# Where tiles lie in the on-chip memory: operands of TensorE at the low end, raw weights and the residual at the high end

## The chip, the cores and the metric

The kernel runs on one core of a Trainium2 chip. The metric is the device time of one execution, in microseconds (us), as the median of several runs. Profiles come from one execution each, recorded by the hardware profiler; their span runs from the first to the last instruction.

## The reference

One decoder layer on x of 256 rows (positions) and 2048 columns, in float32:

```python
x = x + 0.5 * swiglu_ffn(rms_norm(x, ffn1_norm), w_gate, w_up, w_down)   # 2048 -> 5632 -> 2048
z = rms_norm(x, mix_norm) @ w_in                                        # 2048 -> 5120
...   # half of z: width-4 conv, gated linear recurrence, GeLU gate; the rest: gated width-3 conv
x = x + concat(rms_norm(y_lru), rms_norm(y_sc)) @ w_out
x = x + 0.5 * swiglu_ffn(rms_norm(x, ffn2_norm), w_gate, w_up, w_down)
return rms_norm(x, final_norm)
```

with `swiglu_ffn(x) = (silu(x @ w_gate) * (x @ w_up)) @ w_down`. All weights, about 340 MB, are read once.

## The kernel before, in words

**Split products.** The inputs are float32 and TensorE multiplies in a rounded format (float32r). So each operand is split in two: `hi` is its rounded copy (made by ScalarE, `act.copy`), `lo` is what is left (made by VectorE, a subtraction). A product is hi·hi + lo·hi + hi·lo, three matmuls in place of one. A weight block is a *unit* of 512 x 512 numbers: `load` (L155) brings it from HBM into a raw tile of 128 partitions x 4 x 512, 8 KB in each partition; `parts_of` (L169) makes its `hi` and its `lo`, 8 KB each; `multiply` (L194) runs the matmuls. In an FFN and in w_out the rows of x are loaded as the stationary operand, 128 x 128, and the weights are streamed, 512 columns at a time: for one product with a tile of 128 rows a unit gives 8 matmuls with `hi` and 4 with `lo`, 12 in all; 24 if it serves two products. In w_in (`columns`) it is the other way round: the weights are stationary and x is streamed.

**The stages.** FFN 1, the mixer with w_in and w_out, FFN 2. In each FFN the first 512 columns of gate and up are multiplied unit by unit (8 units of 24 matmuls). The other columns go through `seven`, which computes a 2 x 2 arrangement of blocks in seven products instead of eight (Strassen's way): weight blocks are added and subtracted by VectorE in place (`raw_g<-raw_g,raw_g` in the profile), then split and multiplied by sums of the activation blocks. Products over the remaining row blocks (`usual`) are added to the same banks. With two such blocks a `seven` has 7 units of 12 matmuls and 4 of 24, with one it has 7 and 2. Five rounds of gate and up, each a `seven` of two blocks, are followed after the first, third and fifth by `down`: a part of w_down, for two of its four column groups by plain `product` (2 x 3, 2 x 4 and 2 x 4 units of 24), for the other two by a `seven` with one, two and two extra blocks. Between them the hidden activations are transposed by TensorE (`ph`) and split. In the names of the profile `_p` marks one of the seven products, `_x` a `usual` one, and a/c/d/e the bank.

**Order of the work.** Each engine runs its instructions in order. SyncE issues the loads of raw tiles as those tiles come free; the numbers of buffers bound how far the loads and the splitting run ahead of TensorE. Small pieces of other work (transpositions for the next norm, the recurrence) are deferred and handed out by `pump` between units.

**The pools.** All tiles lie in the on-chip memory, 224 KB in each partition, in pools that are opened one after another on one stack, each behind the one before:

- `const`: xres (the residual, 16 KB), the identity, small vectors. L74.
- `raws`: three raw tiles, 24 KB. L75.
- `splits`: two sets of `hi` and `lo`, 32 KB. L76.
- `bigs`: ten tiles of 8 KB, 80 KB: the split activations that TensorE loads as stationary (xT, x, xs, h, yT), and some others. L77.
- `work`: scratch of the norms, some 6 KB. L78.
- then one pool for the stage: in an FFN `ffn1` or `ffn2` with 13 `keep` tiles of 2 KB (sums of banks, activations, and in a `down` the split sums `hs`, which TensorE loads), a third set of `hi` and `lo` with one buffer each (16 KB), and two `kept` raw tiles (16 KB); in the mixer `mixer` and `mixw` in the same place.

While an FFN's pool is open (`extra` isn't empty) every third call of `parts_of` takes the third set. The count, `turn_of["split"]`, runs on from FFN 1 to FFN 2; the mixer uses `splits` alone:

```python
        pool, bufs = splits, 2
        if extra:
            turn_of["split"] += 1
            if turn_of["split"] % 3 == 0:
                pool, bufs = extra[0], 1
```

A raw tile in an FFN goes to `kept` for the first two blocks of a `seven`, and for two of five units of a plain product.

Of the kernel before, what the change touches and what calls it, by code (L numbers as in the profile page):

```python
# [10 lines left out]
F32 = mybir.dt.float32  # L11
# [5 lines left out]
P = 128  # L17
D = 2048
S = 256
FF = 5632  # L20
NT = S // P
# [27 lines left out]
def hybrid_block(ctx: ExitStack, tc: tile.TileContext, a: dict, out: bass.AP):  # L49
# [21 lines left out]
            fn()  # L71
            owed[0] -= cost

    const = ctx.enter_context(tc.tile_pool(name="const", bufs=1))  # L74
    raws = ctx.enter_context(tc.tile_pool(name="raws", bufs=3))  # L75
    splits = ctx.enter_context(tc.tile_pool(name="splits", bufs=2))  # L76
    bigs = ctx.enter_context(tc.tile_pool(name="bigs", bufs=10))  # L77
    work = ctx.enter_context(tc.tile_pool(name="work", bufs=2))  # L78
    psum = ctx.enter_context(tc.tile_pool(name="psum", bufs=8, space=bass.MemoryType.PSUM))

    def bank(name):
# [3 lines left out]
        return ap.bitcast(F32)  # L85


    xres = const.tile([P, NT, D], F32, name="xres")

    def load_x(c):  # L90
        cs = slice(c * CW, (c + 1) * CW)
# [309 lines left out]
        done(0, 0, d, [s1])  # L401

    def ffn(tag, norm, after, opening=False):
        with tc.tile_pool(name=f"ffn{tag}", bufs=1) as fp:
            extra.append(fp)
            turn_of["hold"] = True
            wg, wu, wd = (a[f"ffn{tag}_w_{s}"][0] for s in ("gate", "up", "down"))
# [64 lines left out]
            left = []  # L472
# [169 lines left out]
    def to_mixer(c, t):  # L642
# [3 lines left out]
        else:  # L646
            held["nm"].later(c)

    ffn(1, n1, to_mixer, True)
    nm = held["nm"]  # L650


    with tc.tile_pool(name="mixer", bufs=1) as mp, tc.tile_pool(name="mixw", bufs=2) as mw:
        wgate = {}

        def gate_weights(key, src):
# [218 lines left out]
    def last(c, t):  # L875
# [31 lines left out]
        for engine, begin, end in ((act, 0, 256), (dve, 1536, 2048), (act, 256, 768), (dve, 768, 1536)):  # L907
# [8 lines left out]
            nc.sync.dma_start(ov[:, t, o], xo)  # L916

    ffn(2, n2, last)


# [28 lines left out]
```

## Time and profile before

| what | value |
|---|---|
| median of 3 runs | 1754.29 us (1753.98 to 1757.33) |
| the profiled execution: time, span | 1759.12 us, 1757.3 us |
| granted TensorE clock | 0.998 |
| VectorE busy, ScalarE busy | 1491.3 us, 1050.3 us |
| DMA | 343.24 MB, mean 195 GB/s |

The profile names a tile without its buffer number, so a unit in the third set has the same name as one in `splits`. All helpers' instructions stand at one line, L42, the wrapper that issues them. A row of the timeline gives the start of a group of equal instructions, the time from its first start to its last end, the engine, the operation, the tile written, those read (of a matmul the streamed operand, then the stationary one), the shape and the count. As matmuls overlap at their ends, the pace of a group is the start of the next group less its own start, divided by the count. The last but two columns of a stage's row (`1.00 0.57 195`) are the granted clock, the share of the DMA engines and GB/s; ahead of them stand, for each engine, its busy time and number of instructions.

### The profile page before, as it was taken

The numbers are of one execution on the slowest core, as the hardware profiler recorded it, in microseconds if no ns is written. First come the engines' busy times: TensorE is split into PE (matmuls) and PEld (weight loads), VectorE is DVE, ScalarE is ACT, GpSimd is POOL, SyncE is SP. The second block draws the span as 40 slices with busy tenths as digits, with TensorE's granted clock in tenths as the row PEclk, the third lists the DMA queues.
The fourth block names the chain that finished last, engine by engine and source line by source line (L and its number), as shares of the span: only waits on it lengthen the run. The fifth ranks groups of instructions, "written<-read, shape, count | busy, mean of one in ns | idle before, by whom it ended". The sixth has DMA issues, their size and how long they took to land. (4 is left out here: it accounts for less than half of the span.)

```text
span 1757.3 us, 20323 instructions
## 1 busy us (share of the span) xinstructions
PE 1735.2 (99%) x8031; PEld 1434.5 (82%) x8031; DVE 1491.3 (85%) x1240; ACT 1050.3 (60%) x1366; POOL 6.9 (0%) x32
## 2 busy tenths in 40 slices
PE   8999999999999999999999999999999999999997
PEld 7778788888888888888888888888788888888876
DVE  6998989889789898588986668989799887899885
ACT  7665565655465666565765455656556654556654
POOL 1000000000000000000000000000000000000000
PEclk9999999999999999999999999999999999999999
DMA  8365655575556555456555664575475646555742
GB/s 313 119 231 176 216 192 193 191 263 185 169 198 203 200 195 194 166 169 193 186 180 185 241 204 131 205 247 177 162 248 201 208 145 225 191 192 192 254 172 102
DMA packets 173904, 343.24 MB, mean 195 GB/s; under 512 B 5620, under 2 KB 8048, under 8 KB 173680
## 3 DMA queue, kind: packets, MB, share of 16 engines
q1 hardware_dynamic: 173344, 340.82, 57.3%
q8 instruction: 63, 1.03, 0.2%
q10 hardware_dynamic: 144, 1.05, 0.1%
q14 instruction: 33, 0.27, 0.0%
q0 software_dynamic: 320, 0.07, 0.0%
HBM read 339.82 MB, written 2.10 MB: 195 GB/s over the span
## 5 line engine op out<-in xcount | busy, mean ns | idle before, releaser
L42 PE MATMUL ps_in<-xT_nm,hi_in 128*128 128x512 f32 x640 | 224.0, 395 | 0.0
L42 ACT CAST hi_g_p<-raw_g 128x1024 fp32r<-128x1024 f32 x140 | 142.3, 1049 | 110.8 <-DVE raw_g L42 53.9
L42 DVE TENSOR_TENSOR lo_g_p<-raw_g,hi_g_p 128x2048 fp32r<-128x2048 f32 x70 | 159.7, 2287 | 31.2 <-ACT hi_g_p L42 30.9
L42 ACT CAST hi_u_p<-raw_u 128x1024 fp32r<-128x1024 f32 x140 | 141.1, 1049 | 74.3 <-DVE raw_u L42 27.9
L42 PE MATMUL ps_in<-xT_nm,lo_in 128*128 128x256 f32 x640 | 178.7, 281 | 1.6 <-DVE lo_in L42 1.6
L42 DVE TENSOR_TENSOR lo_u_p<-raw_u,hi_u_p 128x2048 fp32r<-128x2048 f32 x70 | 159.1, 2286 | 19.3 <-ACT hi_u_p L42 19.0
L42 PE MATMUL ps_d<-hi_d,h 128*128 128x512 f32 x704 | 169.5, 392 | 0.0
L42 PEld LDWEIGHTS ps_d<-hi_d,h 128*128 128x128 f32 x704 | 131.5, 188 | 28.2
L42 PEld LDWEIGHTS ps_in<-xT_nm,hi_in 128*128 128x128 f32 x640 | 119.8, 187 | 27.1
L42 ACT CAST hi_d<-raw_d 128x1024 fp32r<-128x1024 f32 x88 | 88.3, 1049 | 69.8 <-PE ps_u_d L42 20.1
L42 DVE TENSOR_TENSOR lo_d<-raw_d,hi_d 128x2048 fp32r<-128x2048 f32 x44 | 100.6, 2291 | 32.0 <-ACT hi_d L42 32.0
L42 PEld LDWEIGHTS ps_in<-xT_nm,lo_in 128*128 128x128 f32 x640 | 120.6, 189 | 2.6 <-DVE lo_in L42 2.4
L42 DVE TENSOR_TENSOR lo_in<-raw_in,hi_in 128x2048 fp32r<-128x2048 f32 x40 | 91.4, 2285 | 32.9 <-ACT hi_in L42 27.6
L42 ACT CAST hi_in<-raw_in 128x1024 fp32r<-128x1024 f32 x80 | 81.6, 1050 | 62.5 <-PE ps_in L42 48.4
L42 ACT CAST hi_d_p<-raw_d 128x1024 fp32r<-128x1024 f32 x84 | 84.3, 1047 | 54.0 <-DVE raw_d L42 38.6
L42 ACT CAST hi_g_x<-raw_g 128x1024 fp32r<-128x1024 f32 x80 | 81.5, 1049 | 43.9 <-PE ps_g_c L42 24.4
L42 DVE TENSOR_TENSOR lo_d_p<-raw_d,hi_d_p 128x2048 fp32r<-128x2048 f32 x42 | 95.5, 2288 | 13.5 <-ACT hi_d_p L42 13.4
L42 ACT CAST hi_u_x<-raw_u 128x1024 fp32r<-128x1024 f32 x80 | 80.5, 1049 | 35.6 <-PE ps_u_c L42 21.2
L42 DVE TENSOR_TENSOR raw_u<-raw_u,raw_u 128x2048 f32<-128x2048 f32 x40 | 91.5, 2290 | 11.4 <-DMA raw_u<-in_ffn_w_up_dram 10.8
L42 DVE TENSOR_TENSOR raw_g<-raw_g,raw_g 128x2048 f32<-128x2048 f32 x40 | 91.4, 2287 | 8.4 <-DMA raw_g<-in_ffn_w_gate_dram 7.9
L42 DVE TENSOR_TENSOR lo_g_x<-raw_g,hi_g_x 128x2048 fp32r<-128x2048 f32 x40 | 91.5, 2286 | 4.4 <-ACT hi_g_x L42 4.3
L42 DVE TENSOR_TENSOR lo_u_x<-raw_u,hi_u_x 128x2048 fp32r<-128x2048 f32 x40 | 91.4, 2285 | 1.0 <-ACT hi_u_x L42 0.3
(347 smaller groups left out, 3602.2 us busy)
## 6 DMA issues: line engine op xcount, KB each, us to landing
raw_u<-in_ffn_w_up_dram SPq DMA_DIRECT2D x88, 1024.0 KB, 5.3
raw_d<-in_ffn_w_down_dram SPq DMA_DIRECT2D x88, 1024.0 KB, 5.1
raw_g<-in_ffn_w_gate_dram SPq DMA_DIRECT2D x87, 1024.0 KB, 5.2
raw_in<-in_w_in_dram SPq DMA_DIRECT2D x40, 1024.0 KB, 5.1
raw_o<-in_w_out_dram SPq DMA_DIRECT2D x16, 1024.0 KB, 5.0
xres<-in_x_dram SPq DMA_DIRECT2D x4, 512.0 KB, 8.1
fin<-in_final_norm_dram ACTq DMA_DIRECT2D x1, 1024.0 KB, 6.5
out_dram<-xres SPq DMA_DIRECT2D x4, 256.0 KB, 2.7
```

The lines of the kernel that those rows point to most:

```text
L42: ins = getattr(self.engine, name)(*args, **kwargs)
```

## The change

The pools get a side. `const`, `splits`, `bigs` and the pools of the stages are stacked from the low end (left), `raws`, `work` and a new pool `stream`, which holds xres alone, from the high end (right). Nothing else is changed: the same tiles, sizes, numbers of buffers and instructions.

```diff
-    const = ctx.enter_context(tc.tile_pool(name="const", bufs=1))
-    raws = ctx.enter_context(tc.tile_pool(name="raws", bufs=3))
-    splits = ctx.enter_context(tc.tile_pool(name="splits", bufs=2))
-    bigs = ctx.enter_context(tc.tile_pool(name="bigs", bufs=10))
-    work = ctx.enter_context(tc.tile_pool(name="work", bufs=2))
+
+    const = ctx.enter_context(tc.tile_pool(name="const", bufs=1, side="left"))
+    splits = ctx.enter_context(tc.tile_pool(name="splits", bufs=2, side="left"))
+    bigs = ctx.enter_context(tc.tile_pool(name="bigs", bufs=10, side="left"))
+    stream = ctx.enter_context(tc.tile_pool(name="stream", bufs=1, side="right"))
+    raws = ctx.enter_context(tc.tile_pool(name="raws", bufs=3, side="right"))
+    work = ctx.enter_context(tc.tile_pool(name="work", bufs=2, side="right"))
...
-    xres = const.tile([P, NT, D], F32, name="xres")
+    xres = stream.tile([P, NT, D], F32, name="xres")
...
-        with tc.tile_pool(name=f"ffn{tag}", bufs=1) as fp:
+        with tc.tile_pool(name=f"ffn{tag}", bufs=1, side="left") as fp:
...
-    with tc.tile_pool(name="mixer", bufs=1) as mp, tc.tile_pool(name="mixw", bufs=2) as mw:
+    with tc.tile_pool(name="mixer", bufs=1, side="left") as mp, tc.tile_pool(name="mixw", bufs=2, side="left") as mw:
```

## The prediction

> **What bounds the kernel now.** I read the busy table, the granted clock, the table by stage, TensorE's waits and then TensorE's timeline.
>
> ```profile
> span 1757.3 us, 20323 instructions
> PE 1735.2 (99%) x8031; PEld 1434.5 (82%) x8031; DVE 1491.3 (85%) x1240; ACT 1050.3 (60%) x1366; POOL 6.9 (0%) x32
> ```
> ```profile
> core 0: 1757.3 us, clock 0.998
> ```
> ```profile
> 50.00:250.00 200.00, 195.53 (x858) 157.81 (x857) 183.60 (x126) 120.13 (x143) 0.00 (x0) 1.00 0.57 195
> 250.00:715.00 465.00, 465.00 (x2074) 382.24 (x2074) 404.57 (x277) 282.45 (x338) 0.00 (x0) 1.00 0.58 196
> 955.00:1038.00 83.00, 83.00 (x383) 69.07 (x383) 58.35 (x74) 43.16 (x67) 0.00 (x0) 1.00 0.62 215
> 1250.00:1668.00 418.00, 417.71 (x1859) 342.88 (x1858) 365.12 (x223) 252.23 (x291) 0.00 (x0) 1.00 0.61 204
> ```
> ```profile
> PE pt_n L42 <- DMA xres<-in_x_dram: 3.3, 1, 3.3
> PE ps_g_c L42 <- DVE x L42: 2.3, 1, 2.3
> ```
>
> TensorE is busy 99% of the span at clock 0.998. From 250 to 715 us it has no idle time at all, while VectorE works 404.57 of 465 us (87%). The longest waits of TensorE are 3.3 and 2.3 us. So time can only be won in the stream of matmuls itself: the diff changes none of them, only where their operands lie. The question is whether a matmul's time depends on that.
>
> **Where things lie.** No view shows addresses; I add up the pools in the order in which the kernel opens them (KB per partition). Before: xres and small constants to 21.5, raws to 45.5, splits 45.5 to 77.5, bigs 77.5 to 157.5, work to 163.3, then the stage's pool: `keep` 163.3 to 189.3, the third set of `hi`/`lo` 189.3 to 205.3, `kept` to 221.3. The matmul's stream (moving operand) is `hi` or `lo`; what is loaded as weights is xT, x, xs, h, yT in bigs, or `hs`, which is `keep`. In an FFN every third call of parts_of takes the third set; w_in and w_out use splits alone. So w_out is a stage in which everything that TensorE multiplies lies below 158 KB. Its matmuls, by start-to-start times (the second column contains a drain that overlaps the next group):
>
> ```profile
> 983.72 3.90 PE L42 MATMUL ps_o<-hi_o,yT 128*128 128x512 f32 x16
> 987.46 1.98 PE L42 MATMUL ps_o<-lo_o,yT 128*128 128x512 f32 x8
> 989.27 3.79 PE L42 MATMUL ps_o<-hi_o,yT 128*128 128x512 f32 x16
> 992.90 1.98 PE L42 MATMUL ps_o<-lo_o,yT 128*128 128x512 f32 x8
> 994.71 3.79 PE L42 MATMUL ps_o<-hi_o,yT 128*128 128x512 f32 x16
> ```
>
> From 989.27 to 994.71 there are 24 matmuls in 5.44 us: 226.7 ns each. The first 24 after a transposition take 5.55. Now the end of the first FFN:
>
> ```profile
> 678.05 2.03 PE L42 MATMUL ps_d_c<-hi_d_p,hs 128*128 128x512 f32 x8
> 679.92 1.10 PE L42 MATMUL ps_d_c<-lo_d_p,hs 128*128 128x512 f32 x4
> 680.85 2.01 PE L42 MATMUL ps_d_d<-hi_d_x,h 128*128 128x512 f32 x8
> 682.70 1.98 PE L42 MATMUL ps_d_a<-hi_d_x,h 128*128 128x512 f32 x8
> ...
> 686.32 2.01 PE L42 MATMUL ps_d_a<-hi_d_p,h 128*128 128x512 f32 x8
> 688.17 1.08 PE L42 MATMUL ps_d_a<-lo_d_p,h 128*128 128x512 f32 x4
> 689.09 2.01 PE L42 MATMUL ps_d_a<-hi_d_x,h 128*128 128x512 f32 x8
> 690.94 1.99 PE L42 MATMUL ps_d_d<-hi_d_x,h 128*128 128x512 f32 x8
> ...
> 694.58 1.98 PE L42 MATMUL ps_d_d<-hi_d_p,h 128*128 128x512 f32 x8
> 696.39 1.07 PE L42 MATMUL ps_d_d<-lo_d_p,h 128*128 128x512 f32 x4
> 697.30 3.84 PE L42 MATMUL ps_d<-hi_d,h 128*128 128x512 f32 x16
> 700.98 1.99 PE L42 MATMUL ps_d<-lo_d,h 128*128 128x512 f32 x8
> 702.81 1.03 PE L42 MATMUL pt_nm<-ident,xres 128*128 128x128 f32 x8
> 703.60 3.89 PE L42 MATMUL ps_d<-hi_d,h 128*128 128x512 f32 x16
> ```
>
> An FFN calls parts_of 171 times (worked out below), so I count back from its end: the unit at 697.30 is the 168th and in the third set, the one at 686.32 the 165th, and in between (689.09, 694.58) stand two in splits. The third-set unit at 686.32 takes 2.77 us for 12 matmuls; the splits unit at 694.58 takes 2.72. The unit behind it (689.09, in splits) takes 5.49 us for 24 where w_out needs 5.44: the stream needs some ten matmuls to get back to its pace. The third-set unit of 24 at 697.30 takes 5.51. The units at 678.05, with `hs` as weights at 163 KB or above, take 2.80, or 233 ns per matmul, though their stream comes from splits. TensorE shows no wait in these rows. So this trace has a far stretch, from at latest 163 KB, that TensorE reads more slowly, by stream or by weights, and a near one, to at least 157 KB for weights and 77 KB for streams, that runs at 226.7 ns.
>
> **The change, part by part.** The left end holds 5.5 KB of constants, splits to 37.5, bigs to 117.5, `keep` to 143.5, the third set 143.5 to 159.5, `kept` to 175.5. xres, raws and work go to the top 46 KB.
>
> Third set: how many units? One `seven` with two extra blocks has 7 units of 12 matmuls and 4 of 24; with one, 7 and 2. Each FFN runs ten of the first for gate and up, then sevens with one, two and two blocks in the downs, 8 units of 24 in the opening and 6 + 8 + 8 in the plain products: 91 of 12 and 80 of 24, 171. A third of it in two FFNs: 61 of 12 and 53 of 24. The unit of 12 costs 2.77 - 2.72 = 0.05 us itself and 0.05 in the unit behind it: 61 x 0.10 = 6.1. The unit of 24 costs 5.51 - 5.44 = 0.07, and the same 0.05 behind it: 53 x 0.12 = 6.4. Together **12.5 us**.
>
> `hs`: six downs with four such products of 12 matmuls; 2.80 - 2.72 = 0.08 us each. A third of the 24 is already in the sum above: 16 x 0.08 = **1.3 us**. Sum 13.8; these differences are read to 0.01 us, so 12 to 15.
>
> What of it doesn't reach the end: from 50 to 250 us TensorE is idle for 4.5 us and VectorE busy for 183.6 of 200, so there the pace is set by the splitting, not by TensorE. 858 matmuls at 17.6 per unit are 49 units, 16 in the third set: 16 x 0.11 = 1.8 us given back. The first 50 us and the last stage's few waits I put at 0.5, likewise by their third-set units. Elsewhere VectorE goes from 87% to 88%, with no TensorE wait now; I take another 0.7 off for that, between 0 and 2. Net 13.8 - 1.8 - 0.5 - 0.7 = **10.8 us**.
>
> xres at the far end: TensorE reads it in 96 transpositions, 12 groups of 8. Far tiles are transposed already, `ph`:
>
> ```profile
> 1573.71 1.03 PE L42 MATMUL ph<-ident,u_g 128*128 128x128 f32 x8
> 1574.50 2.10 PE L42 MATMUL ps_u_d<-hi_u_p,x 128*128 128x512 f32 x8
> 1576.44 1.08 PE L42 MATMUL ps_u_d<-lo_u_p,x 128*128 128x512 f32 x4
> ```
>
> 8 of them last 0.79 us (1573.71 to 1574.50), as the 8 of near xres at 702.81 do (to 703.60). The 8 matmuls behind the far ones take 1.94 us, 0.13 above 8 x 226.7 ns; behind near ones (983.72) it was 0.11 over 24. So some 0.02 us per group: 12 groups lose 0.3 us, and the 176 `ph` transpositions, which become near, gain the like: 0.
>
> raws at the far end: does a far tile cost ACT, VectorE or the DMA more? w_in has only near raws; the FFNs mix near and far (`kept`, third set):
>
> ```profile
> L42 DVE TENSOR_TENSOR lo_g_p<-raw_g,hi_g_p 128x2048 fp32r<-128x2048 f32 x70 | 159.7, 2287 | 31.2 <-ACT hi_g_p L42 30.9
> L42 DVE TENSOR_TENSOR lo_in<-raw_in,hi_in 128x2048 fp32r<-128x2048 f32 x40 | 91.4, 2285 | 32.9 <-ACT hi_in L42 27.6
> L42 ACT CAST hi_in<-raw_in 128x1024 fp32r<-128x1024 f32 x80 | 81.6, 1050 | 62.5 <-PE ps_in L42 48.4
> L42 ACT CAST hi_d<-raw_d 128x1024 fp32r<-128x1024 f32 x88 | 88.3, 1049 | 69.8 <-PE ps_u_d L42 20.1
> raw_g<-in_ffn_w_gate_dram SPq DMA_DIRECT2D x87, 1024.0 KB, 5.2
> raw_in<-in_w_in_dram SPq DMA_DIRECT2D x40, 1024.0 KB, 5.1
> ```
>
> 2287 against 2285 ns, 1049 against 1050, 5.2 against 5.1 us: nothing. The order of instructions, the numbers of buffers and which pool reuses which room stay as they are, since the stage pools still lie on one stack; I count no new wait.
>
> The median of before is 1754.29; the profiled execution is 1759.1 with a span of 1757.3, 5 us above it. I take the difference from the median: 1754.3 - 10.8 = **1743.5**.
>
> **Rivals.** (A, the forecast, 0.75) Far streams and far weights were slow, and all but xres is near now; own range 1740 to 1748.
>
> (B, 0.10) The third set stays slow at 143.5 to 159.5 KB: no row shows a 512-column stream back to back from above 77 KB; or its pace comes from lying in one pool with the tiles that ACT and VectorE write, or from its single buffer. For it: only weights are seen fast up to 157 KB. Against it: `hs` has no single buffer and no shared split, and is slow as well. Then only `hs` gains, 1.3 us and its recoveries (16 x 0.04): 1752.4.
>
> (C, 0.07) The layout means nothing: what I read as distance is the place of the units in a cycle of three, and TensorE's pace comes out as before, 1754.3. Against it: 2.80 us for `hs` outside the cycle, and w_out without such a cycle has every unit at 5.44. The Trainium skill has a rule for this case: SBUF — State Buffer, section "Who interferes with whom", says that TensorE and ScalarE never wait for anybody at the memory, and names no price for an address. By that rule the sum is zero; the trace here speaks against it, with 2.77 and 2.80 us against 2.72.
>
> (D, slower, 0.08) TensorE reads stream and weights at once, and the low end now packs both into 5.5 to 117.5 KB. If the two reads hinder each other when they lie close, the near units get the pace of `hs`, 233 instead of 226.7 ns. The two FFNs have 6,024 such matmuls, 4,016 of them from splits: 4,016 x 6.6 ns = 26.5 us lost against 10.8 won, 1770. It decides from 10.8 / 0.0066 = 1,640 matmuls on. For it: the far units have `hs` and the third set together above 163 KB. Against it: splits and bigs adjoin already in before, and run at 226.7.
>
> **Chances.** A measurement here can tell about 0.2% (3.5 us) from no change. Faster: A and a little of B, 0.76. Same: the rest of B and C, 0.16. Slower: D, 0.08. A and B hold 0.85, so the range goes from 1740, where nothing is given back, to 1753.
>
> **What would show it.** In the after trace third-set units take 2.72 us for 12 and 5.44 for 24, like those in splits; `hs` products 2.72; w_out and w_in keep their pace; VectorE's 2287 and ACT's 1049 ns stay. Third-set units at 2.77 with `hs` at 2.72 would be B; w_out's 5.44 grown would be D; TensorE waits grown by many us would say that the splitting took the gain.

## The result, and the profile after

The changed kernel takes 1747.68 us (median of 5 runs, 1746.44 to 1749.81). The kernel before, timed beside it, takes 1757.33 us (5 runs, 1753.98 to 1759.02). The ratio is 0.9946, with a 95% interval of 0.9935 to 0.9957: 9.65 us faster. The profiled execution took 1749.81 us; the first two rows are from its page, the third from the view of the cores.

```profile
span 1748.0 us, 20323 instructions
PE 1726.0 (99%) x8031; PEld 1436.3 (82%) x8031; DVE 1490.3 (85%) x1240; ACT 1049.1 (60%) x1366; POOL 6.9 (0%) x32
```
```profile
core 0: 1748.0 us, clock 0.997
```

The instructions are the same in number, and the 8,031 matmuls come in the same order. VectorE and ScalarE are as busy as before (1491.3 and 1050.3 us there). The span is 9.3 us shorter and TensorE's busy time 9.2. The table by stage, for the stretches that the prediction shows of before:

```profile
50.00:250.00 200.00, 194.40 (x856) 158.72 (x855) 183.41 (x126) 119.77 (x143) 0.00 (x0) 0.99 0.57 195
250.00:715.00 465.00, 465.00 (x2097) 385.80 (x2097) 407.35 (x281) 284.51 (x342) 0.00 (x0) 1.00 0.58 197
955.00:1038.00 83.00, 83.00 (x383) 69.06 (x382) 55.93 (x64) 40.68 (x59) 0.00 (x0) 1.00 0.64 215
1250.00:1668.00 418.00, 418.00 (x1879) 346.79 (x1878) 368.22 (x231) 252.10 (x293) 0.00 (x0) 1.00 0.62 211
```

TensorE is busy without a gap from 250 to 715 us, as before, but starts 2,097 matmuls there in place of 2,074. In w_out (955 to 1038 us) it is 383 in both. From 50 to 250 us it is 856 against 858: nothing is won there in this execution. TensorE's timeline at the end of the first FFN, the same instructions as the prediction shows of before:

```profile
674.30 1.98 PE L42 MATMUL ps_d_c<-hi_d_p,hs 128*128 128x512 f32 x8
...
677.02 1.98 PE L42 MATMUL ps_d_d<-hi_d_x,h 128*128 128x512 f32 x8
...
682.47 1.98 PE L42 MATMUL ps_d_a<-hi_d_p,h 128*128 128x512 f32 x8
...
685.18 1.98 PE L42 MATMUL ps_d_a<-hi_d_x,h 128*128 128x512 f32 x8
...
690.62 1.98 PE L42 MATMUL ps_d_d<-hi_d_p,h 128*128 128x512 f32 x8
...
693.35 3.79 PE L42 MATMUL ps_d<-hi_d,h 128*128 128x512 f32 x16
...
698.79 1.04 PE L42 MATMUL pt_nm<-ident,xres 128*128 128x128 f32 x8
699.59 1.62 PE L42 MATMUL ps_d<-hi_d,h 128*128 128x512 f32 x6
```

The unit in the third set takes 2.71 us (682.47 to 685.18; 2.77 before), the one with `hs` 2.72 (674.30 to 677.02; 2.80), the one in `splits` 2.73 (690.62 to 693.35), the third-set unit of 24 matmuls 5.44 (693.35 to 698.79; 5.51), and the 24 behind the third-set unit 5.44 (685.18 to 690.62; 5.49). Every unit now has w_out's pace.

**Where the 9.3 us went.** The matmuls of the two traces can be paired one by one. I take the time from each start to the next start, call what exceeds one matmul in gaps over 280 ns a wait, and the rest pace (us, after less before; stretches by the times of before):

| stretch | in all | waits | pace |
|---|---|---|---|
| start to 250 | +0.2 | +2.0 | -1.8 |
| 250 to 715, FFN 1 | -4.2 | 0.0 | -4.2 |
| 715 to 1038, mixer | -0.3 | -1.2 | +0.9 |
| 1038 to 1250, FFN 2 begins | -0.9 | +0.7 | -1.6 |
| 1250 to 1668, FFN 2 | -3.8 | 0.0 | -3.8 |
| 1668 to the end | -0.3 | +0.5 | -0.8 |

The FFNs won 12.2 us of pace, and 9.3 us arrived. In the long stretches nothing came back. In the first 250 us all of it did, but 1.6 of the 2.0 us are matmuls that ran at half pace for a while (shown below) and not idle time. (In the mixer a wait cut below 280 ns counts as pace, so its two columns are to be read together.)

### The profile page after: what moved, and what is told of

The parts are those of the page before. It is cut to its first block, busy times and chain, and to the rows that moved or that the text cites. A ratio compares the mean times of both kernels' runs of the same rounds, so it can differ in the third digit from the quotient of the medians.

```text
span 1748.0 us, 20323 instructions
## 1 busy us (share of the span) xinstructions
PE 1726.0 (99%) x8031; PEld 1436.3 (82%) x8031; DVE 1490.3 (85%) x1240; ACT 1049.1 (60%) x1366; POOL 6.9 (0%) x32
## 5 line engine op out<-in xcount | busy, mean ns | idle before, releaser
L42 DVE TENSOR_TENSOR lo_g_p<-raw_g,hi_g_p 128x2048 fp32r<-128x2048 f32 x70 | 159.3, 2286 | 30.3 <-ACT hi_g_p L42 30.2
L42 ACT CAST hi_u_p<-raw_u 128x1024 fp32r<-128x1024 f32 x140 | 141.0, 1049 | 71.7 <-DVE raw_u L42 28.7
L42 DVE TENSOR_TENSOR lo_u_p<-raw_u,hi_u_p 128x2048 fp32r<-128x2048 f32 x70 | 159.1, 2286 | 18.2 <-ACT hi_u_p L42 17.8
L42 ACT CAST hi_d<-raw_d 128x1024 fp32r<-128x1024 f32 x88 | 88.4, 1049 | 68.1 <-PE ps_u_d L42 22.4
L42 ACT CAST hi_d_p<-raw_d 128x1024 fp32r<-128x1024 f32 x84 | 84.4, 1049 | 53.3 <-DVE raw_d L42 39.8
L42 DVE TENSOR_TENSOR lo_d_p<-raw_d,hi_d_p 128x2048 fp32r<-128x2048 f32 x42 | 95.4, 2286 | 11.9 <-ACT hi_d_p L42 11.8
L42 DVE TENSOR_TENSOR raw_g<-raw_g,raw_g 128x2048 f32<-128x2048 f32 x40 | 91.4, 2287 | 9.0 <-DMA raw_g<-in_ffn_w_gate_dram 8.5
```

The lines of the kernel that those rows point to most:

```text
L42: ins = getattr(self.engine, name)(*args, **kwargs)
```

## The experiments

Each kernel is compared with runs of the kernel before that were timed beside it on the same chip; ratios are to those.

**1. TensorE alone, one address after another (`probe`).** The theory so far is the prediction's: distance, a far stretch that TensorE reads more slowly. Its rival puts the pace down to a unit's neighbours, not to its address. The kernel leaves out the layer and only multiplies: 106 tiles of 2 KB stand one behind the other from 10 to 222 KB, and groups of 24 matmuls take their stream, their weights or both from each address.

```diff
+    for k in steps:
+        run("stream", near, tiles[k], 24)     # then ("weights", tiles[k], near), ("both", ...)
+    for _ in range(8):
+        run("swapfar", near, far, 12)
+        run("swapnear", near, near, 24)
```

> This kernel leaves the whole layer out: it fills 106 tiles of 2 KB that lie one behind the other from 10 to 222 KB, and then TensorE alone runs groups of 24 matmuls of 512 columns, once with the stream, once with the weights and once with both read from one tile after the other, then 12 far and 24 near ones in turn, then pairs of 512 and 256 columns as in w_in. Theory (distance): with nothing else at work the pace is 226.7 ns below about 160 KB and changes to 229 or more above it for streams, to about 233 for weights, at an address between 157.5 and 163.3 KB. Rival (neighbours: far tiles were slow because ScalarE, VectorE and the DMA wrote beside them): 226.7 ns at every address, since nothing writes here.

TensorE's timeline; `t_ba` lies at 30 KB, `t_jg` and `t_jh` at 202 and 204 KB:

```profile
34.16 5.60 PE L69 MATMUL ps_stream<-t_ba 128*128 128x512 f32 x24
39.60 5.60 PE L69 MATMUL ps_stream<-t_bi,t_ba 128*128 128x512 f32 x24
```
```profile
268.08 5.60 PE L69 MATMUL ps_stream<-t_jg,t_ba 128*128 128x512 f32 x24
273.52 5.60 PE L69 MATMUL ps_stream<-t_jh,t_ba 128*128 128x512 f32 x24
```
```profile
942.64 2.88 PE L69 MATMUL ps_swapfar<-t_jg,t_ba 128*128 128x512 f32 x12
945.36 5.60 PE L69 MATMUL ps_swapnear<-t_ba 128*128 128x512 f32 x24
950.80 2.88 PE L69 MATMUL ps_swapfar<-t_jg,t_ba 128*128 128x512 f32 x12
```

24 matmuls take 5.44 us with the stream at 30 KB (34.16 to 39.60) and 5.44 at 202 KB (268.08 to 273.52), and so at every address tried from 14 to 222 KB, by stream, by weights and by both. Twelve far ones take 2.72 (942.64 to 945.36), and the 24 near ones behind them 5.44: no recovery. An address far up costs TensorE nothing by itself. What was left for distance was an effect that needs the other engines.

**2. The new order without sides (`low_splits`).** The pools in the order of the change on one stack: `splits` and `bigs` are as low as in the changed kernel, the FFN pool is back at 163.3 KB.

```diff
-    splits = ctx.enter_context(tc.tile_pool(name="splits", bufs=2, side="left"))
+    splits = ctx.enter_context(tc.tile_pool(name="splits", bufs=2))
...   # and so every pool
```

> One stack as before, but splits and bigs are moved down by 40 KB, and xres, raws and work come behind them; the pool of the stage lies where it lay before the change (third set 189 to 205 KB, hs from 163 KB). Theory (distance): only tiles above about 160 KB are slow, and they are still there, so the time is that of the kernel before, ratio 1.000 (0.998 to 1.002), third-set units at 2.77 us for 12. Rival (what counts is that raws, written by the DMA, no longer lie beside splits, or that splits and bigs lie lower): the gain of the change is kept, ratio 0.994 to 0.996.

1757.87 against 1756.63 us, ratio 1.0007 (0.9997 to 1.0016): no gain. The third-set unit:

```profile
685.81 2.01 PE L42 MATMUL ps_d_a<-hi_d_p,h 128*128 128x512 f32 x8
...
688.58 2.01 PE L42 MATMUL ps_d_a<-hi_d_x,h 128*128 128x512 f32 x8
```

2.77 us, as before. So the place of the FFN pool seems to matter, and that of `splits` and `bigs` not. That is what distance foretells, against what the first run says.

**3. The sides exchanged (`mirror`).** Now `splits` (189 to 221 KB) and `bigs` (109 to 189 KB) lie far, the third set near (77 to 93 KB).

```diff
-    splits = ctx.enter_context(tc.tile_pool(name="splits", bufs=2, side="left"))
+    splits = ctx.enter_context(tc.tile_pool(name="splits", bufs=2, side="right"))
...   # left and right exchanged for every pool
```

> All sides of the changed kernel exchanged: constants, splits (189 to 221 KB) and bigs (109 to 189 KB) at the high end, the third set at 77 to 93 KB and keep below 77 KB, xres and raws at the low end. Theory (distance): now the 228 units in splits are slow and the 114 in the third set fast, so 228 units lose 0.05 to 0.07 us each (13.5), 114 recoveries 0.05 each (5.7), and weights in the upper 30% of bigs up to 12 more: 20 to 32 us above the changed kernel, ratio to before 1.006 to 1.013; w_out slow as well. Rival (the third set is slow for its pool or its single buffer, not for its address): third-set units at 2.77 us for 12 and splits at 2.72 as before, ratio 1.000.

1746.06 against 1756.63, ratio 0.9944 (0.9927 to 0.9960). Distance had 1.006 to 1.013 and its rival no change: both are wrong. The first two rows are the third-set unit, the others a unit in `splits` and what follows it:

```profile
680.89 1.98 PE L42 MATMUL ps_d_a<-hi_d_p,h 128*128 128x512 f32 x8
...
683.62 1.98 PE L42 MATMUL ps_d_a<-hi_d_x,h 128*128 128x512 f32 x8
...
689.05 1.98 PE L42 MATMUL ps_d_d<-hi_d_p,h 128*128 128x512 f32 x8
...
691.77 3.79 PE L42 MATMUL ps_d<-hi_d,h 128*128 128x512 f32 x16
```

2.73 near and 2.72 far. Both kinds are fast with everything at the far end, so neither distance nor neighbours can be the cause. What the slow layouts have in common stands in the bytes that I had rounded to KB. A new theory: **the place of an operand within a small block of bytes**. Before, `raws` starts at byte 22,048, `splits` at 46,624, `bigs` at 79,392 and the FFN pool at 167,264. Divided by 256 the first three leave 32, the FFN pool leaves 96, since `work` is 5,952 bytes long, which is 23 x 256 + 64. The tiles of these pools are multiples of 256 long, so the third set and `hs` stand 64 bytes off from the other operands of the 512-column products. In `low_splits` it is 96 against 32 again. After the change `splits` starts at 5,664, `bigs` at 38,432, the FFN pool at 120,352: all leave 32, for `work` went to the other end. In `mirror` the pools from which the FFNs, w_in and w_out multiply all leave 64, and in the first probe all tiles left 128, which is why it could show nothing.

**4. TensorE alone, with offsets (`probe_phase`).** Again without the layer. Stream and weights stand at 32 bytes (modulo 512), and eleven further sets at 0, 64, 96 and so on; plain runs of 24 first, then units as in the kernel, two in the base set and one in another.

```diff
+    for c in other:      # a 64, b 96, c 128, d 160, e 192, f 256, g 288, h 352, i 384, k 448, ...
+        run("stream", big[:, 0, :P], other[c][0][:, 0, :])
+    for c in other:
+        run("weights", other[c][0][:, 0, :P], hi[:, 0, :])
+    for c in other:
+        for n in range(3):
+            for k in range(2):
+                unit("near", big, hi, lo, k)
+            unit("other", big, *other[c], n % 2)
```

> Leaves the whole layer out: TensorE alone runs units as the kernel does (8 matmuls with hi, 4 with lo, weights from big), with one set of hi and lo at the same place within 512 bytes as big (32 bytes) and eleven others at 64, 96, 128, 160, 192, 256, 288, 352, 384, 448 and 0, put in turn as the third set is; then the same sets as weights, and the pairs of 512 and 256 columns of w_in. New theory (phase: a unit is slow where stream and weights start at different places within 512 bytes, as in the kernel before the third set and hs at 352 and all else at 32): units with the set at 352 take 2.77 us for 12 matmuls, with 0.05 behind them, sets with other differences show which differences count, and near units by themselves take 2.72. Rival (it takes what the other engines or the whole kernel do beside it): every unit takes 2.72 us.

TensorE's timeline, the sweep of the stream (sets f to i) and then the units with set h (352, which is 96 modulo 256, the kernel's own case). In the second fence a row that is a single matmul marks where a unit begins:

```profile
56.62 5.76 PE L89 MATMUL ps_stream<-hi_f,big 128*128 128x512 f32 x24
62.22 5.63 PE L89 MATMUL ps_stream<-hi_g,big 128*128 128x512 f32 x24
67.69 5.67 PE L89 MATMUL ps_stream<-hi_h,big 128*128 128x512 f32 x24
73.20 2.04 PE L89 MATMUL ps_stream<-hi_i,big 128*128 128x512 f32 x8
```
```profile
390.45 0.40 PE L94 MATMUL ps_other<-hi_h,big 128*128 128x512 f32 x1
...
393.22 0.40 PE L94 MATMUL ps_near<-hi,big 128*128 128x512 f32 x1
...
395.99 0.39 PE L94 MATMUL ps_near<-hi,big 128*128 128x512 f32 x1
...
398.71 0.40 PE L94 MATMUL ps_other<-hi_h,big 128*128 128x512 f32 x1
```

The unit in set h takes 2.77 us (390.45 to 393.22), the unit behind it 2.77 as well, the next 2.72: the kernel's own numbers, with no other engine at work. So neither ScalarE, VectorE nor the DMA has a part in it. The same unit with set g (288, which is 32 modulo 256) takes 2.72 (365.97 to 368.69). All the sweeps, in us per 24 matmuls (each set changes places with the one before it, so a group starts with some matmuls at a mixed pace):

| the set's remainder less the base set's, modulo 256 | stream there | weights there | stream and weights both there |
|---|---|---|---|
| 0 (set g) | 5.47 | 5.44 | 5.47 |
| 64 (b and h) | 5.51 | 5.60 | 5.47, 5.49 |
| others | 5.60 to 5.61 | 5.57 to 5.62 | 5.46 to 5.50 |

A matmul takes 226.7 ns where stream and weights leave the same remainder, whichever that is; 229.4 where the stream stands 64 above the weights; 232 to 234 in every other case. The difference counts with its sign: weights 64 above the stream make a difference, stream less weights, of 192. Where the difference is the same, the times from start to start repeat in the same order, whichever operand was moved: 237, 231, 232 ns with the stream in set c and with the weights in set e, 96 both times. After a change of the remainders up to ten matmuls lie in between (224 to 241 ns), even where both change together: that makes the 5.46 to 5.50 in the last column, whose later matmuls run at 226.7. The third set's 5.51 is the 64 in the stream, and the `hs` products' 2.80 for 12 (233 ns) is the 64 in the weights, a difference of 192, here 5.60 for 24. The Trainium skill, SBUF — State Buffer, section "Who interferes with whom", gives TensorE two read ports, one for the moving operand and one for the weights, and calls them independent; here the trace differs, since the pace hangs on how stream and weights lie to each other: 5.44 against 5.51 to 5.62 us. Whether it is at the ports that the two meet, no run shows.

**5. 192 idle bytes in the kernel before (`before_shift`).** An unused tile ahead of the stage pools moves the FFN pool from remainder 96 to 32. It stays at the far end, and nothing else of the change is made.

```diff
     work = ctx.enter_context(tc.tile_pool(name="work", bufs=2))
+    shift = ctx.enter_context(tc.tile_pool(name="shift", bufs=1))
...
+    nc.gpsimd.memset(shift.tile([P, 48], F32, name="shift"), 0.0)
```

> The kernel before with one idle tile of 192 bytes between the pools work and those of the stages, so that the FFN's pool lies 192 bytes higher, at the far end still, and starts at 32 within 512 bytes as splits and bigs do. Theory (phase): all the gain of the change comes from this alone, ratio 0.993 to 0.996. Rival (where the pool lies): nothing, ratio 1.000.

1746.06 against 1757.59, ratio 0.9938 (0.9918 to 0.9958): the whole gain, from 192 bytes that nobody reads.

```profile
681.99 1.98 PE L42 MATMUL ps_d_a<-hi_d_p,h 128*128 128x512 f32 x8
...
684.71 1.98 PE L42 MATMUL ps_d_a<-hi_d_x,h 128*128 128x512 f32 x8
```

The third set, at some 189 KB as before, takes 2.72.

**6. 320 idle bytes in the changed kernel (`after_shift`).** The reverse: all stays at the low end, and the FFN pool goes from 32 to 352 (96 modulo 256).

```diff
     bigs = ctx.enter_context(tc.tile_pool(name="bigs", bufs=10, side="left"))
+    shift = ctx.enter_context(tc.tile_pool(name="shift", bufs=1, side="left"))
...
+    nc.gpsimd.memset(shift.tile([P, 80], F32, name="shift"), 0.0)
```

> The changed kernel with one idle tile of 320 bytes between bigs and the pools of the stages, so that the FFN's pool starts at 352 within 512 bytes, as in the kernel before, and else lies where the change put it. Theory (phase): the gain is gone, ratio to before 0.999 to 1.001, third-set units at 2.77 us for 12. Rival (where the pool lies): the gain stays, 0.994 to 0.996.

1756.62 against 1757.59, ratio 0.9997 (0.9988 to 1.0007): the gain is gone.

```profile
686.86 2.01 PE L42 MATMUL ps_d_a<-hi_d_p,h 128*128 128x512 f32 x8
...
689.63 2.01 PE L42 MATMUL ps_d_a<-hi_d_x,h 128*128 128x512 f32 x8
```

2.77 us again, with the third set at 144 KB.

**7. A worse offset (`before_64`).** By the probe a difference of 32 costs more than one of 64. The kernel before with 224 idle bytes has 32.

```diff
+    nc.gpsimd.memset(shift.tile([P, 56], F32, name="shift"), 0.0)
```

> The kernel before with an idle tile of 224 bytes ahead of the stages' pools: the FFN's pool starts at 64 within 256 bytes, all else that TensorE multiplies at 32, a difference of 32 in place of 64. Theory (phase within 256 bytes, each difference with the price that TensorE alone showed): third-set units of 12 take 2.81 us instead of 2.77, of 24 5.60 instead of 5.51, and the unit behind them 0.01 less, so the kernel becomes slower than before: 61 x 0.03 + 53 x 0.08 = 6 us, ratio 1.002 to 1.005. Rival (any difference costs the same): ratio 1.000.

1763.15 against 1757.50, ratio 1.0033 (1.0020 to 1.0045): slower, as expected.

```profile
687.96 2.03 PE L42 MATMUL ps_d_a<-hi_d_p,h 128*128 128x512 f32 x8
...
690.76 2.01 PE L42 MATMUL ps_d_a<-hi_d_x,h 128*128 128x512 f32 x8
...
698.96 3.90 PE L42 MATMUL ps_d<-hi_d,h 128*128 128x512 f32 x16
...
704.56 1.04 PE L42 MATMUL pt_nm<-ident,xres 128*128 128x128 f32 x8
```

2.80 for 12 and 5.60 for 24, the probe's numbers.

**8. 256 or 512 (`before_288`).** The kernel before with 448 idle bytes: the FFN pool at 288, which equals 32 modulo 256 but not modulo 512.

```diff
+    nc.gpsimd.memset(shift.tile([P, 112], F32, name="shift"), 0.0)
```

> The same with an idle tile of 448 bytes: the FFN's pool at 288 within 512 bytes, which is 32 within 256. Theory (the place within 256 bytes counts): all fast, ratio 0.993 to 0.996. Rival (the place within 512 bytes counts): slow, ratio 1.000 or above.

1746.72 against 1757.50, ratio 0.9939 (0.9925 to 0.9953), and the third-set unit takes 2.72 us (680.16 to 682.88). The block is 256 bytes.

**9. Another common remainder (`after_64`).** In `mirror`, where all stands at 64, w_in's matmuls looked a little quicker, and in the probe pairs like w_in's, whose two operands both move, took 346.7 ns at some remainders and 353 at others. So the changed kernel with 32 idle bytes in `const`: all at 64.

```diff
+    nc.gpsimd.memset(const.tile([P, 8], F32, name="shift"), 0.0)
```

> The changed kernel with an idle tile of 32 bytes in const: all that TensorE multiplies in the FFNs and in w_in lies at 64 within 256 bytes instead of 32. Theory: in the FFNs nothing changes, as only the difference counts (2.72 us for 12); in w_in, whose pairs took 346.7 ns at 64 and 352.8 at 32 with TensorE alone and about 350.7 and 347.7 in the changed kernel and its mirror, 640 pairs gain 3 to 4 ns each: 2 to 2.6 us, ratio to before 0.992 to 0.995, 0.001 under the change's 0.9946. Rival (w_in's pace hangs on something else that the mirror moved): as the changed kernel.

1746.31 against 1757.50, ratio 0.9935 (0.9921 to 0.9949), whose interval overlaps the change's own. Of the 2 to 2.6 us expected in w_in little came. Its matmuls with `hi`, in the view of the groups, in the changed kernel, in `after_64` and in `mirror`:

```profile
L42 PE MATMUL ps_in<-xT_nm,hi_in 128*128 128x512 f32 x640 | 224.7, 396 | 0.0
```
```profile
L42 PE MATMUL ps_in<-xT_nm,hi_in 128*128 128x512 f32 x640 | 224.1, 395 | 0.0
```
```profile
L42 PE MATMUL ps_in<-xT_nm,hi_in 128*128 128x512 f32 x640 | 222.8, 393 | 0.0
```

At most 0.6 us of busy time moved with the remainder. The probe's pairs add to one bank and the kernel's to four in turn; whether that is why the probe's gain isn't found here wasn't tried. What makes w_in slightly quicker in `mirror` stays open.

## Why the prediction was right, and which step was wrong

**The bound: right.** TensorE's stream sets the time. In the long stretches without idle time the pace won, 4.2 and 3.8 us, arrived in full.

**The readings: right.** 2.77, 2.80 and 5.51 against 2.72 and 5.44, and the recovery in the unit behind, are real. The probe gives the same figures with TensorE alone.

**The reason: wrong.** The step that failed is the sentence "this trace has a far stretch, from at latest 163 KB, that TensorE reads more slowly, by stream or by weights, and a near one". There is no far stretch: 5.44 us for 24 at every address from 14 to 222 KB (run 1), all fast with everything far (run 3), the gain had at 189 KB (run 5) and lost again at 144 KB (run 6). The cause is the place of the stream within 256 bytes, relative to that of the weights. The prediction added up the pools in KB to one decimal and so rounded away the 64 bytes that decide. Most rows of before fit both causes, since only one pool was far, and the same pool was off. But six of the 24 `hs` products take their stream from the third set, and there both operands lie far and leave the same remainder. The unit ahead of the one at 678.05 is such a one, in before:

```profile
675.29 2.01 PE L42 MATMUL ps_d_a<-hi_d_p,hs 128*128 128x512 f32 x8
677.14 1.08 PE L42 MATMUL ps_d_a<-lo_d_p,hs 128*128 128x512 f32 x4
678.05 2.03 PE L42 MATMUL ps_d_c<-hi_d_p,hs 128*128 128x512 f32 x8
```

It takes 2.76 us, its last four matmuls 0.91, which is w_out's pace; the one behind it, with only the weights far, takes 2.80 and 0.93 (679.92 to 680.85). If distance were the cause, two far operands could not be quicker than one; the prediction counted these units as slow. The sign was in the trace of before and was overlooked. So the number came out right by luck: the change moved `work`, the one pool whose length is no multiple of 256, out from between; a change by the same idea with another odd pool left between would have won nothing, as runs 2 and 6 show.

**The sum: slightly high, and one term right by luck.** 13.8 us of pace were forecast, within 12 to 15, and 12.2 measured. 3.0 were to be given back; 2.9 were (9.3 of 12.2 arrived, the mixer's 0.3 counted in). The share from the start to 250 us was 1.8 of pace, and it was lost, as much as foreseen, but for the most part not to the splitting, as the prediction had it. The window from 66 to 75 us, before and then after:

```profile
66.00:75.00 9.00, 6.72 (x34) 5.23 (x33) 8.93 (x9) 5.43 (x9) 0.00 (x0) 1.00 0.33 117
```
```profile
66.00:75.00 9.00, 6.71 (x30) 5.27 (x29) 8.93 (x9) 5.42 (x9) 0.00 (x0) 0.90 0.38 117
```

The granted clock falls to 0.90, and the timeline, after and then before, shows why:

```profile
73.29 1.65 PE L42 MATMUL ps_g_c<-hi_g_x,x 128*128 128x512 f32 x3 [2.29 <-DVE x L42]
74.73 2.44 PE L42 MATMUL ps_g_a<-hi_g_p,xs 128*128 128x512 f32 x6
```
```profile
73.42 0.96 PE L42 MATMUL ps_g_c<-hi_g_x,x 128*128 128x512 f32 x3 [2.28 <-DVE x L42]
74.22 2.03 PE L42 MATMUL ps_g_a<-hi_g_p,xs 128*128 128x512 f32 x8
```

Behind a wait of 2.29 us three matmuls take 1.44 us; in before, behind a wait of 2.28, the same three take 0.80. In all six matmuls run at 427 ns start to start, and one ahead of them and one behind (590 and 335 ns) lie in between: some 1.6 us lost. The wait is the same. From 70 to 80 us the granted clock is 0.83 in the changed kernel, `before_shift`, `after_64` and also `after_shift`, where the gain is gone, and 1.00 in before, `low_splits`, `mirror`, `before_64` and `before_288`: the lower clock isn't tied to the gain. It lasts 3.41 us each time (73.23 to 76.65 in the changed kernel). An estimate from the nine traces: counted in steps of 3.41 us from the start of each trace's first clock record, 2.2 us or more of the wait lie within one step in the four executions with the lower clock, 2.0 or less in the five others. No run varied that. `mirror` and `before_288`, from 50 to 250 us:

```profile
50.00:250.00 200.00, 195.13 (x865) 159.04 (x864) 184.93 (x127) 120.81 (x144) 0.00 (x0) 1.00 0.56 195
50.00:250.00 200.00, 195.10 (x866) 159.25 (x865) 185.45 (x126) 121.18 (x144) 0.00 (x0) 1.00 0.56 195
```

With the clock at 1.00 TensorE starts 865 and 866 matmuls there, 858 in before. Paired with before as above, the stretch up to 250 us is 1.6 and 2.1 us shorter (`low_splits`, which has no gain, differs by 0.5): in these two executions most of the pace won there did arrive, and the step "so there the pace is set by the splitting, not by TensorE" doesn't hold.

**The time.** 1747.68 is 4.2 us above the forecast 1743.5: 3.0 of that is the median of before, 1757.33 in this comparison in place of 1754.29, and 1.2 the difference itself, 9.65 in place of 10.8.

**The costs put at nothing: right.** From the page after: the splitting and casting of far raw tiles cost what they did, and so do the loads (5.2 us for `raw_g`, 5.1 for `raw_in`, in both pages).

```profile
L42 DVE TENSOR_TENSOR lo_g_p<-raw_g,hi_g_p 128x2048 fp32r<-128x2048 f32 x70 | 159.3, 2286 | 30.3 <-ACT hi_g_p L42 30.2
...
L42 ACT CAST hi_d<-raw_d 128x1024 fp32r<-128x1024 f32 x88 | 88.4, 1049 | 68.1 <-PE ps_u_d L42 22.4
```

2286 ns against 2287, 1049 against 1049. The transpositions of xres, now far, take 0.80 us for eight (698.79 to 699.59 in the timeline after; 0.79 before).

**The rivals.** B fell: the third set is fast at 143.5 to 159.5 KB with its single buffer and its pool. C fell as to time, but the rule it rested on was half right: no other engine hinders TensorE, and address alone means nothing. D fell: with stream and weights packed into 5.5 to 159.5 KB every unit has w_out's pace.

## What to carry to other kernels

Give every pool from which TensorE reads the same remainder modulo 256 bytes: count the pools' starts in bytes, and pad scratch pools that stand between to a multiple of 256 (192 idle bytes are worth 0.6% of this kernel). Where two groups of equal matmuls differ by 1 to 3% without a wait, look at the operands' places within 256 bytes first. A theory about the layout is cheaply tried by moving one pool by a small unused tile.

## What the runs showed of the hardware

- The pace of back-to-back 128x512 float32r matmuls hangs on the start address of the stream less that of the weights, modulo 256 bytes: 226.7 ns at 0, 229.4 at 64, 232 to 234 at 32, 96, 128, 160, 192 and 224. After a change up to ten matmuls run in between. Why a difference of 64 costs least is open, and differences that are no multiple of 32 weren't tried.
- From 14 to 222 KB the address has no effect of its own on this pace, and casts, subtractions and loads beside it have none either (2.77 us alone and in the kernel).
- A wait of 2.3 us was followed by 3.41 us of TensorE at about half pace (in the changed kernel six matmuls at 427 ns) in four of the nine profiled kernels that hold the layer, and not in the other five, behind the same matmuls.
